# Merging small triangular inverses: one link of the dependent chain replaced, and banks of their own for two batches

## The chip, the cores and the metric

The kernel runs on one core of one Trainium2 chip. The metric is device time in microseconds (us) of that core. TensorE (PE) multiplies and writes PSUM, eight banks of 512 float32 columns on 128 partitions; ScalarE (ACT) and VectorE (DVE) read PSUM and copy to SBUF; GpSimd (POOL) works on SBUF alone; SyncE (SP) issues most DMAs.

## The reference, cut to what matters

Two layers on 512 tokens of width 1024: an RWKV-7 time mixer and a spatial gating unit, each followed by a SwiGLU FFN, with RMS norms around all. The change lies in the RWKV-7 mixer. Its recurrence, per head of width 64:

```
S_t = S_{t-1} diag(w_t) + (S_{t-1} a_t) b_t^T + v_t k_t^T ;   y_t = S_t r_t
```

The kernel computes it in chunks of 64 tokens. Within a chunk the tokens depend on each other through a strictly triangular 64x64 matrix L of a and b; the kernel needs (I - L)^-1 of every head and chunk, 16 heads x 8 chunks = 128 inverses. Everything is float32.

## The kernel before, in words

The 16 heads are taken in four batches b of four heads: two pairs q, and in a pair two heads hd, one on partitions 0 to 63, one on 64 to 127. With eight chunks that is 16 matrices u per hd and batch. A list `PLAN` (P0 E0 P1 ... F3 N0 B2 N1 B3 S2 N2 S3 N3) gives the order in which the program's steps are written: P projections, E the elementwise part, F `front` (products lm and bkt between the chunk's vectors, masked by GpSimd into LA, MV, BX), B `back` (the inverses, then products mp and gh that apply them), V values, S `scan` over the chunks (products us and Yp, small copies su), N group norm, bonus and gate. The order in which each engine really gets its instructions is decided by a planner that simulates the whole program while it is built, so steps of several batches interleave. It obeys data dependences, and dependences through buffers: `self.bank(tag, name)` hands out the PSUM banks of a tag in turn, and a new tile in a bank waits for the readers of the tile that had it before. In this phase tag pt is banks 3 and 4, pl is 1 and 2 (lm, bkt, mvt), mp is 5.

In `back`, LX and Dm give the inverses of the 16x16 diagonal blocks by a loop on VectorE (lines 1064 to 1070); Dn and Dt are two transposed forms of them (lines 1073, 1074). mvt are transposes of MV, copied to MVt (lines 1079 to 1084). Then the blocks are merged. With x = 0 or 1 for the upper or lower 32 rows of a matrix, `quarters` are the four (hd, x), each on 32 partitions of its own:

- Qp (line 1090), four quarters: off-diagonal part of L times Dn. Qs = Qp + I on VectorE (line 1093).
- Np (line 1099), x = 0 only, and Tp (line 1102), four quarters: Dt with Qs. Tp holds the 32x32 inverses, copied to the diagonal of bdT by VectorE and ScalarE (line 1107); Np is copied to Dn2 by ScalarE (line 1105).
- Q2p (line 1113): the 32x32 block of L below the diagonal times Dn2; copied to Q2 (lines 1116, 1117).
- T2p (line 1122): Q2 times the lower inverse in bdT, the off-diagonal 32x32 block; copied to bdT (line 1126). The last two copies are kept as `merged0`, `merged1`: loads for the out-projection are issued behind those of batch 3.

After that mp (line 1131) multiplies bdT with MVt, and gh (line 1138) with BX; VectorE adds gh into MV (lines 1140, 1141), which `scan` reads. One product of two 32x32 float32 tiles appears as two matmul instructions in the profile. In the profile's names Dn2 is Dn, Q2 is Q, Dn is hn, and id32 is id.

Of the kernel before, what the change touches and what calls it, by code (L numbers as in the profile page):

```python
# [13 lines left out]
P = 128  # L14
# [119 lines left out]
class Trunk:  # L134
# [553 lines left out]
    def rwkv(self, x0):  # L688
        nc, i, tc = self.nc, self.i, self.tc
        v, a, g = nc.vector, nc.scalar, nc.gpsimd  # L690
        mm = nc.tensor.matmul
        with ExitStack() as ctx:
# [352 lines left out]
            def back(b, o):  # L1045
# [40 lines left out]
                quarters = [(64 * hd + 32 * x, hd, x) for hd in q2 for x in q2]  # L1086
                Qp = self.bank("pt", "Qp")
# [6 lines left out]
                Np = self.bank("pt", "Np")  # L1094
                Tp = self.bank("pt", "Tp")
                for u in range(16):
                    for z, hd, x in quarters:
                        if x == 0:
                            mm(Np[z:z + 32, u * 32:(u + 1) * 32], Dt[z:z + 32, u, x, :], Qs[z:z + 32, u, :], start=True, stop=True)
                for u in range(16):  # L1100
                    for z, hd, x in quarters:
                        mm(Tp[z:z + 32, u * 32:(u + 1) * 32], Qs[z:z + 32, u, :], Dt[z:z + 32, u, x, :], start=True, stop=True)
                Dn2 = el("Dn2", (P, 16, 32))
                for z in (0, 64):
                    a.copy(Dn2[z:z + 32].rearrange("p u s -> p (u s)"), Np[z:z + 32, :])
                for z, hd, x in quarters:
                    (a.copy if x else v.tensor_copy)(bdT[z:z + 32, :, hd, 32 * x:32 * x + 32],
                                                     Tp[z:z + 32, :].rearrange("p (u t) -> p u t", t=32))

                Q2p = self.bank("pt", "Q2p")  # L1110
                for u in range(16):
                    for z in (0, 64):
                        mm(Q2p[z + 32:z + 64, u * 32:(u + 1) * 32], LAu[z:z + 32, u, 32:64], Dn2[z:z + 32, u, :],
                           start=True, stop=True)
                Q2 = el("Q2", (P, 16, 32))
                a.copy(Q2[32:64].rearrange("p u s -> p (u s)"), Q2p[32:64, :])
                v.tensor_copy(Q2[96:128].rearrange("p u s -> p (u s)"), Q2p[96:128, :])
                T2p = self.bank("pt", "T2p")
                for u in range(16):
                    for hd in q2:  # L1120
                        z = 64 * hd
# [348 lines left out]
```

## Time and profile before

| | |
|---|---|
| three runs, us | 1311.30, 1311.77, 1318.54 (median 1311.77) |
| profiled execution, its own time, us | 1310.66 |
| its span, us | 1309.0 |
| PE busy | 1255.0 us, 96%, 9692 matmuls |
| PE weight loads busy | 1090.5 us, 83% |
| DVE busy | 991.3 us, 76% |
| ACT busy | 739.0 us, 56% |
| POOL busy | 150.2 us, 11% |
| four merges in the span | from 221.0, 269.0, 313.6 and 359.4 us |

Busy PE is not PE at its peak, since the ends of pipelined matmuls are modelled. PEclk is the granted TensorE clock as a share of full speed. A bracket such as "[1.98 <-issue]" gives the idle time of the engine before an instruction and what ended it; "issue" is a wait for nothing that the profile shows. The releaser of a wait is inferred.

### The profile page before, as it was taken

The numbers are of one execution on the slowest core, as the hardware profiler recorded it, in microseconds if no ns is written. First come the engines' busy times: TensorE is split into PE (matmuls) and PEld (weight loads), VectorE is DVE, ScalarE is ACT, GpSimd is POOL, SyncE is SP. The second block draws the span as 40 slices with busy tenths as digits, with TensorE's granted clock in tenths as the row PEclk, the third lists the DMA queues.
The fourth block names the chain that finished last, engine by engine and source line by source line (L and its number), as shares of the span: only waits on it lengthen the run. The fifth ranks groups of instructions, "written<-read, shape, count | busy, mean of one in ns | idle before, by whom it ended". The sixth has DMA issues, their size and how long they took to land.

```text
span 1309.0 us, 24482 instructions
## 1 busy us (share of the span) xinstructions
PE 1255.0 (96%) x9692; PEld 1090.5 (83%) x9692; DVE 991.3 (76%) x1613; ACT 739.0 (56%) x1303; POOL 150.2 (11%) x300
## 2 busy tenths in 40 slices
PE   5999999989899999999999999999999999999997
PEld 3667799878777698999997878878898999998876
DVE  6976766467957779768779976575689777789985
ACT  7986785576454454445456556653464454455553
POOL 0000284566100012000000000020002000000000
PEclk9999999989989999999999999999999999999999
DMA  5137595322143225243344413242440433344322
GB/s 164 33 97 176 144 227 158 86 72 62 60 117 120 81 66 161 72 123 115 92 149 138 125 59 118 91 139 90 142 114 1 129 109 107 109 129 145 113 65 81
DMA packets 218819, 143.24 MB, mean 109 GB/s; under 512 B 67872, under 2 KB 193360, under 8 KB 218704
## 3 DMA queue, kind: packets, MB, share of 16 engines
q1 hardware_dynamic: 217408, 136.96, 36.6%
q0 software_dynamic: 1296, 4.72, 1.1%
q8 instruction: 76, 1.25, 0.4%
q14 instruction: 39, 0.32, 0.1%
HBM read 128.02 MB, written 13.63 MB: 108 GB/s over the span
## 4 chain that ended last, share of the span: by engine, by line
PE 67%; DVE 8%; issue 2%; ACT 1%; DMA 1%; SPq 0%; POOL 0%; DVEq 0%; ACTq 0%
PE acc L208 25%; PE Q L208 10%; PE Z L208 7%; PE gu L208 6%; PE R L208 6%; PE u L208 3%; PE gh L1138 1%; DVE wlo L184 1%; PE Yp L1180 1%; DVE wsum L413 1%; PE lm L1023 1%; PE mp L1131 1%; PE ptr L283 1%; DMA wq<-in_ffn_w_up_dram 1%; DVE x L339 1%
## 5 line engine op out<-in xcount | busy, mean ns | idle before, releaser
L208 PE MATMUL Q<-bc,whi 128*128 128x256 f32 x816 | 147.5, 281 | 2.9 <-ACT hn L457 2.9
L184 DVE TENSOR_TENSOR wlo<-wraw,whi 128x1024 fp32r<-128x1024 f32 x83 | 103.3, 1247 | 58.7 <-ACT whi L183 57.6
L208 PE MATMUL acc<-whi,ablk 128*128 128x512 f32 x448 | 141.5, 395 | 2.7 <-DVE acc L642 2.7
L183 ACT CAST whi<-wraw 128x1024 fp32r<-128x1024 f32 x83 | 86.9, 1049 | 92.7 <-PE acc L208 16.6
L208 PEld LDWEIGHTS Q<-bc,whi 128*128 128x128 f32 x816 | 125.6, 189 | 3.7 <-ACT hn L457 3.5
L183 ACT CAST whi<-wsum 128x1024 fp32r<-128x1024 f32 x68 | 71.0, 1051 | 86.3 <-PE Q L208 29.2
L208 PE MATMUL Q<-bc,wlo 128*128 128x256 f32 x408 | 114.5, 281 | 0.0
L208 PE MATMUL gu<-hT,whi 128*128 128x256 f32 (+1 forms) x480 | 109.1, 322 | 0.0
L208 PEld LDWEIGHTS acc<-whi,ablk 128*128 128x128 f32 x448 | 84.1, 188 | 23.3 <-ACT hn L640 1.8
L208 PE MATMUL Z<-bc,whi 128*128 128x256 f32 x544 | 99.9, 281 | 1.6 <-DVE bc L184 1.6
L208 PE MATMUL R<-bc,whi 128*128 128x256 f32 x544 | 99.0, 280 | 0.0
L184 DVE TENSOR_TENSOR wlo<-wsum,whi 128x1024 fp32r<-128x1024 f32 x68 | 82.1, 1220 | 18.9 <-ACT whi L183 17.7
L183 ACT CAST whi<-wq 128x1024 fp32r<-128x1024 f32 x51 | 53.5, 1049 | 70.2 <-PE R L208 22.9
L208 PE MATMUL acc<-wlo,ablk 128*128 128x512 f32 x224 | 88.7, 396 | 2.2 <-DVE wlo L184 2.2
L208 PEld LDWEIGHTS gu<-hT,whi 128*128 128x128 f32 x480 | 79.4, 188 | 8.1 <-issue 1.0
L208 PEld LDWEIGHTS Z<-bc,whi 128*128 128x128 f32 x544 | 84.1, 189 | 1.8 <-DVE bc L184 1.8
L184 DVE TENSOR_TENSOR wlo<-wq,whi 128x1024 fp32r<-128x1024 f32 x51 | 64.3, 1262 | 26.7 <-ACT whi L183 26.6
L208 PEld LDWEIGHTS R<-bc,whi 128*128 128x128 f32 x544 | 84.0, 188 | 0.4
L208 PE MATMUL proj<-xsp,whi 128*128 128x512 f32 x256 | 82.5, 401 | 1.3 <-ACT r L832 1.3
L208 PE MATMUL Z<-bc,wlo 128*128 128x256 f32 x272 | 76.6, 282 | 1.7 <-DVE wlo L184 1.7
L208 PEld LDWEIGHTS Q<-bc,wlo 128*128 128x128 f32 x408 | 77.2, 190 | 0.0
L208 PE MATMUL R<-bc,wlo 128*128 128x256 f32 x272 | 76.7, 282 | 0.0
(377 smaller groups left out, 3196.1 us busy)
## 6 DMA issues: line engine op xcount, KB each, us to landing
wc<-in_ffn_w_down_dram SPq DMA_DIRECT2D x38, 512.0 KB, 3.6
wq<-in_ffn_w_gate_dram SPq DMA_DIRECT2D x68, 256.0 KB, 4.1
wq<-in_ffn_w_up_dram SPq DMA_DIRECT2D x68, 256.0 KB
wraw<-in_rwkv_w_rkv_dram SPq DMA_DIRECT2D x24, 512.0 KB, 5.1
wraw<-in_sgu_w_in_dram SPq DMA_DIRECT2D x16, 512.0 KB, 4.2
wraw<-in_ffn_w_gate_dram SPq DMA_DIRECT2D x10, 512.0 KB, 4.5
wraw<-in_ffn_w_up_dram SPq DMA_DIRECT2D x10, 512.0 KB
x<-in_x_dram SPq DMA_DIRECT2D x8, 512.0 KB, 3.8
```

Source lines behind the costliest of these rows:

```text
L183: self.nc.scalar.copy(hi, src)
L184: self.nc.vector.tensor_tensor(lo, src, hi.bitcast(F32), op=ALU.subtract)
L208: self.nc.tensor.matmul(out, l, r, start=start, stop=stop, skip_group_check=resumed)
L283: self.nc.tensor.transpose(pt[:, j * P:(j + 1) * P], xt[:, kt * P:(kt + 1) * P], self.ident)
L339: v.scalar_tensor_tensor(xts[tt][:, c], f, y[:, 0:1], xts[tt][:, c], op0=ALU.mult, op1=ALU.add)
L413: v.tensor_tensor(s, x, y, op=ALU.add)
L1023: mm(lm[:, cc * P:(cc + 1) * P], st[:, cc].rearrange("p n t -> p (n t)"), mv[:, cc, :, hd, :], start=True, stop=True)
L1131: mm(mp[:, cc * P:(cc + 1) * P], bdT[:, q * NC + 4 * hh + cc].rearrange("p h t -> p (h t)"), mt[:, cc, :], start=True, stop=True)
L1138: mm(gh[:, cc * P:(cc + 1) * P], mt[rows, cc, :], bx[rows, 0:2, cc, :], start=True, stop=True)
L1180: mm(yp[yr, yc], MV[hh, q][:, cc, 1, hd, :], su[:, q, hd, :], start=True, stop=True)
```

## The change

The products are written in another order. A group Gp = Dn^T with the lower-left 32x32 block of L (x = 0 only) needs nothing of Qs and replaces Np; its copy is G, copied by ScalarE, or by both engines in batches 2 and 3. Q2p becomes G times Qs. Tp is cut into two calls of `turned(x)`, 32 products each: x = 1 ahead of Q2p, x = 0 after T2p; `placed(x, ...)` copies each to bdT, head 0 by ScalarE and head 1 by VectorE. So the dependent groups are Qp, Q2p, T2p where they were Qp, Np, Q2p, T2p. The number of products (224 a batch) and of PSUM reads (11 a batch) stays.

In batches 2 and 3 (`apart`) each group but Qp takes two banks, one for each head: Gp, Q2p and the x = 0 half of T from tag pl, the x = 1 half and T2p from tag pt. In batches 0 and 1 both heads share one bank of tag pt, as before.

```diff
+                tops = [(hd, 64 * hd) for hd in q2]
+                flat2 = lambda t: t.rearrange("p u s -> p (u s)")
+                apart = b >= 2
+
+                def pair(name, tag):
+                    if apart:
+                        return [self.bank(tag, name) for _ in tops]
+                    return [self.bank("pt", name)] * 2
+
+                def copies(dst, src):
+                    for hd, z in tops:
+                        last = (v.tensor_copy if hd else a.copy)(dst(hd, z), src(hd, z))
+                        o["merged" + str(hd)] = last
+
+                def turned(x):
+                    Tp = pair("Tp", "pt" if x else "pl")
+                    for u in range(16):
+                        for hd, z in tops:
+                            z += 32 * x
+                            mm(Tp[hd][z:z + 32, u * 32:(u + 1) * 32], Qs[z:z + 32, u, :], Dt[z:z + 32, u, x, :], start=True, stop=True)
+                    return Tp
+
+                def placed(x, Tp):
+                    at = slice(32 * x, 32 * x + 32)
+                    copies(lambda hd, z: bdT[z + 32 * x:z + 32 * x + 32, :, hd, at],
+                           lambda hd, z: Tp[hd][z + 32 * x:z + 32 * x + 32].rearrange("p (u t) -> p u t", t=32))
+
...
-                Np = self.bank("pt", "Np")
-                Tp = self.bank("pt", "Tp")
+                Gp = pair("Gp", "pl")
                 for u in range(16):
-                    for z, hd, x in quarters:
-                        if x == 0:
-                            mm(Np[z:z + 32, u * 32:(u + 1) * 32], Dt[z:z + 32, u, x, :], Qs[z:z + 32, u, :], start=True, stop=True)
+                    for hd, z in tops:
+                        mm(Gp[hd][z:z + 32, u * 32:(u + 1) * 32], Dn[z:z + 32, u, 0, :], LAu[z:z + 32, u, 32:64], start=True, stop=True)
+                G = el("G", (P, 16, 32))
+                for hd, z in tops:
+                    (v.tensor_copy if hd and apart else a.copy)(flat2(G[z:z + 32]), Gp[hd][z:z + 32, :])
+                T1 = turned(1)
+                Q2p = pair("Q2p", "pl")
                 for u in range(16):
-                    for z, hd, x in quarters:
-                        mm(Tp[z:z + 32, u * 32:(u + 1) * 32], Qs[z:z + 32, u, :], Dt[z:z + 32, u, x, :], start=True, stop=True)
-                Dn2 = el("Dn2", (P, 16, 32))
-                for z in (0, 64):
-                    a.copy(Dn2[z:z + 32].rearrange("p u s -> p (u s)"), Np[z:z + 32, :])
-                for z, hd, x in quarters:
-                    (a.copy if x else v.tensor_copy)(bdT[z:z + 32, :, hd, 32 * x:32 * x + 32],
-                                                     Tp[z:z + 32, :].rearrange("p (u t) -> p u t", t=32))
-                Q2p = self.bank("pt", "Q2p")
+                    for hd, z in tops:
+                        mm(Q2p[hd][z + 32:z + 64, u * 32:(u + 1) * 32], G[z:z + 32, u, :], Qs[z:z + 32, u, :], start=True, stop=True)
+                placed(1, T1)
+                Q2 = el("Q2", (P, 16, 32))
+                copies(lambda hd, z: flat2(Q2[z + 32:z + 64]), lambda hd, z: Q2p[hd][z + 32:z + 64, :])
+                T2p = pair("T2p", "pt")
                 for u in range(16):
-                    for z in (0, 64):
-                        mm(Q2p[z + 32:z + 64, u * 32:(u + 1) * 32], LAu[z:z + 32, u, 32:64], Dn2[z:z + 32, u, :],
+                    for hd, z in tops:
+                        mm(T2p[hd][z:z + 32, u * 32:(u + 1) * 32], Q2[z + 32:z + 64, u, :], bdT[z + 32:z + 64, u, hd, 32:64],
                            start=True, stop=True)
-                Q2 = el("Q2", (P, 16, 32))
-                a.copy(Q2[32:64].rearrange("p u s -> p (u s)"), Q2p[32:64, :])
-                v.tensor_copy(Q2[96:128].rearrange("p u s -> p (u s)"), Q2p[96:128, :])
-                T2p = self.bank("pt", "T2p")
...
+                placed(0, turned(0))
+                copies(lambda hd, z: bdT[z:z + 32, :, hd, 32:64], lambda hd, z: T2p[hd][z:z + 32].rearrange("p (u t) -> p u t", t=32))
```

More of the change, by code (lines that the diff above doesn't have):

```diff
@@ L1114, in back @@
                            start=True, stop=True)
-                Q2 = el("Q2", (P, 16, 32))
-                a.copy(Q2[32:64].rearrange("p u s -> p (u s)"), Q2p[32:64, :])
-                v.tensor_copy(Q2[96:128].rearrange("p u s -> p (u s)"), Q2p[96:128, :])
-                T2p = self.bank("pt", "T2p")
-                for u in range(16):
-                    for hd in q2:
-                        z = 64 * hd
-                        mm(T2p[z:z + 32, u * 32:(u + 1) * 32], Q2[z + 32:z + 64, u, :], bdT[z + 32:z + 64, u, hd, 32:64],
-                           start=True, stop=True)
@@ L1124, in back @@
-                for hd, cp in ((0, a.copy), (1, v.tensor_copy)):
-                    z = 64 * hd
-                    o["merged" + str(hd)] = cp(bdT[z:z + 32, :, hd, 32:64], T2p[z:z + 32, :].rearrange("p (u t) -> p u t", t=32))
+                placed(0, turned(0))
+                copies(lambda hd, z: bdT[z:z + 32, :, hd, 32:64], lambda hd, z: T2p[hd][z:z + 32].rearrange("p (u t) -> p u t", t=32))
                 for hh, q in units:
```

## The prediction

> **What bounds the kernel now.** I read the page first: its span, and the chain of work that ended last.
>
> ```profile
> span 1309.0 us, 24482 instructions
> ...
> PE 67%; DVE 8%; issue 2%; ACT 1%; DMA 1%; SPq 0%; POOL 0%; DVEq 0%; ACTq 0%
> ```
>
> The profiled execution took 1310.66 us by its own clock against this span of 1309.0, so 1.7 us lie around the span. The chain is two thirds TensorE (PE), so a microsecond on PE's path counts and one on another engine counts only where PE waits for it. Next, the busy time by stage: each row gives the stretch, its length, busy time with instruction count of PE, PE weight loads, VectorE (DVE), ScalarE (ACT) and GpSimd, then the granted PE clock, the DMA share and GB/s.
>
> ```profile
> 213.00:412.00 199.00, 185.38 (x3128) 162.12 (x3128) 132.02 (x294) 113.17 (x268) 70.37 (x169) 0.94 0.29 85
> 412.00:440.00 28.00, 24.66 (x150) 18.10 (x146) 20.51 (x40) 12.75 (x25) 0.00 (x0) 1.00 0.44 132
> 440.00:1309.00 869.00, 850.60 (x5365) 761.54 (x5364) 686.52 (x1041) 446.45 (x729) 34.81 (x31) 1.00 0.35 105
> ```
>
> The edited function runs in the first row's stretch. PE stands 199.00 - 185.38 = 13.6 us there, and the granted clock averages 0.94, worth another 0.06 x 199 = 11.9 us. The FFN and SGU stretch of 869 us contains none of the edited instructions, and its PE is 98% busy. So the change can matter by what it does to those two sums, and by work it adds to PE. The four merges, from the first product Qp to the first mp, and what follows the last:
>
> ```profile
> 220.90:237.90 17.00, 15.34 (x513) 14.64 (x512) 4.97 (x7) 5.57 (x13) 4.66 (x11) 0.90 0.11 35
> 269.00:287.80 18.80, 14.38 (x512) 13.14 (x512) 9.28 (x12) 13.14 (x33) 9.23 (x23) 0.91 0.23 57
> 313.60:340.50 26.90, 24.08 (x583) 20.29 (x581) 18.65 (x39) 21.03 (x54) 15.17 (x37) 0.94 0.24 73
> 359.40:375.50 16.10, 13.30 (x514) 12.27 (x513) 6.02 (x13) 8.32 (x19) 0.41 (x2) 0.74 0.19 55
> 375.50:412.00 36.50, 36.50 (x273) 29.31 (x273) 25.87 (x55) 16.11 (x34) 0.69 (x1) 0.97 0.49 145
> ```
>
> In the four, PE stands 1.66, 4.42, 2.82 and 2.80 us (length less the first busy column), 11.7 in all; the clock costs 0.10 x 17.0 + 0.09 x 18.8 + 0.06 x 26.9 + 0.26 x 16.1 = 9.2. The **ceiling of any gain** is therefore near 21 us, 1.6%. After the fourth merge PE is busy without a gap to 412 us, so what is won or lost before 375.5 passes straight on. The fourth merge, in order of time (start, length, engine, line, operation, count, and in brackets the idle time before it):
>
> ```profile
> 359.41 1.43 PE L1090 MATMUL Qp<-hn,LA 32*32 32x32 f32 x128
> ...
> 361.45 0.68 DVE L1093 TENSOR_TENSOR Qs<-Qp,id 128x512 f32<-128x512 f32 x1
> ...
> 362.19 1.16 PE L1099 MATMUL Np<-Qs,Dt 32*32 32x32 f32 x61 [0.51 <-DVE Qs L1093]
> ...
> 363.43 1.16 ACT L1105 COPY Dn<-Np 32x512 f32<-32x512 f32 x2 [0.57 <-PE Np L1099]
> ...
> 363.68 1.46 PE L1102 MATMUL Tp<-Dt,Qs 32*32 32x32 f32 x122 [0.23 <-issue]
> ...
> 365.19 0.68 DVE L1107 COPY bdT<-Tp 32x512 f32<-32x512 f32 x1 [2.87 <-PE Tp L1102]
> 365.90 0.58 ACT L1107 COPY bdT<-Tp 32x512 f32<-32x512 f32 x1 [1.31 <-DVE bdT L1107]
> 366.51 0.69 DVE L1107 COPY bdT<-Tp 32x512 f32<-32x512 f32 x1 [0.64 <-ACT bdT L1107]
> 367.23 1.80 PE L1113 MATMUL Q2p<-Dn,LA 32*32 32x32 f32 x59 [1.98 <-issue]
> ...
> 369.07 0.58 ACT L1116 COPY Q<-Q2p 32x512 f32<-32x512 f32 x1 [2.59 <-PE Q2p L1113]
> ...
> 370.02 0.70 DVE L1117 COPY Q<-Q2p 32x512 f32<-32x512 f32 x1
> ...
> 371.46 1.91 PE L1122 MATMUL T2p<-bdT,Q 32*32 32x32 f32 x62
> ...
> 373.41 0.57 ACT L1126 COPY bdT<-T2p 32x512 f32<-32x512 f32 x1 [0.96 <-PE T2p L1122]
> ...
> 374.02 0.69 DVE L1126 COPY bdT<-T2p 32x512 f32<-32x512 f32 x1 [2.16 <-ACT bdT L1126]
> ...
> 375.48 2.08 PE L1131 MATMUL mp<-MVt,bdT 128*128 128x128 f32 x8
> ```
>
> Two things are to be seen. The dependent groups are four: Qp, Np, Q2p, T2p, each followed by a copy out of PSUM. And the copies alternate: ACT's at 365.90 begins when DVE's ended, DVE's at 366.51 when ACT's did, DVE's at 374.02 when ACT's at 373.41 was through. The view of waits from 213 to 412 us has this as a rule, with PE's unexplained pauses beside it (engine, what waited for what, us in total, times, longest):
>
> ```profile
> DVE bdT L1126 <- ACT bdT L1126: 7.1, 2, 4.9
> ...
> PE Q2p L1113 <- issue: 3.7, 3, 2.0
> ...
> ACT bdT L1107 <- DVE bdT L1107: 3.8, 3, 1.9
> ...
> DVE bdT L1107 <- ACT bdT L1107: 2.0, 3, 0.7
> PE Tp L1102 <- issue: 1.8, 2, 1.6
> ```
>
> **The change, part by part.** *Work on PE.* Before and after a batch issues 7 x 32 products: Np's 32 go, Gp's 32 come, and Tp's 64 become two calls of 32. But a group's time hardly depends on its count: Qp, 128 instructions over four quarters, takes 1.43 us, Tp's 122 take 1.46, and Np, with half the count in two quarters, still 1.16. Splitting Tp therefore costs 2 x 1.16 - 1.46 = +0.86 a batch, 3.4 us in four if PE has no slack. If it falls into the pauses called "issue" (3.7 + 1.8 = 5.5 us, which sit inside Tp and Q2p, runs of hundreds of small products), it costs nothing. Ends: 0 and 3.4; I take 0 in the chains below, where the groups are already counted one by one, and 0 in batch 0, whose 1.66 us idle covers it.
>
> Those pauses I keep at their length, since the count of small products does not change. The Trainium skill, "Runtime: NRT & Kernel Launch", section "Instruction fetch mechanics", says that instructions come in blocks of 256 and that crossing a block is mostly hidden. That speaks against pauses that recur by count; by it the 1.98 us of the fourth merge need not come back and the time would be 2 us lower. The trace cannot say whether these pauses are fetches.
>
> *The chain, shared banks (batches 0 and 1).* Before, by the rows above: Qp 1.43, Qs 0.68, Np 1.16, Tp 1.46 (beside the two Dn2 copies, 1.16), Q2p at Np's 1.16, its copies 0.58 + 0.70, T2p 1.16, its copies 0.57 + 0.69: 9.6. After: Qp 1.43, Gp 1.16 (Qs runs under it), T1 1.16 (G's two ACT copies under it), Q2p 1.16, copies 1.28 in turn, T2p 1.16, then T0 1.16, which needs Q2p's bank and so cannot fill the copies' wait, and its copies 0.58 + 0.69: 9.8. (T1 and T0 are the two halves of Tp.) G's copies cost up to 1.16 a batch if something else keeps ScalarE from them under T1. The step saved behind Np comes back as T0 at the end: **0**. Bounds: -4.42 if all of batch 1's idle time goes, +1.7 if both batches pay the split.
>
> *The chain, own banks (batches 2 and 3).* Each head's copy has its engine and bank, so a pair takes 0.70 instead of about 1.27, and T0 has banks of its own and fills the wait for Q2. Qp 1.43, Gp 1.16, T1 1.16, Q2p 1.16, T0 1.16 (over Q2's 0.70), T2p 1.16, copies 0.69: 7.9, **-1.7** against 9.6. That presupposes that the alternation is due to the bank and not to the common destination (bdT, Q2). Two engines do write one tile at once:
>
> ```profile
> 308.56 0.76 ACT L1031 COPY BX<-lm 64x256 f32<-64x256 f32 x2 [1.47 <-DVE MV L1140]
> 308.59 0.83 POOL L1018 COPY BX<-ident 64x256 f32<-64x256 f32 x2 [3.52 <-DVE MV L1140]
> ```
>
> Both waited for the same release, the VectorE reader of BX, and ran side by side into that tile; what they don't share is a PSUM bank.
>
> In batch 3 nothing stands in the way, and I take the -1.7 whole. In batch 2 the new products' bank tag does. Gp, Q2p and T0 take tag pl, whose two banks also serve the next batch's lm and bkt and this batch's mvt, all asked for earlier in the program:
>
> ```profile
> 319.71 0.57 PE L1099 MATMUL Np<-Qs,Dt 32*32 32x32 f32 x24
> ...
> 336.12 0.57 ACT L1084 COPY MVt<-mvt 128x512 f32<-128x512 f32 x1
> 336.58 0.57 ACT L1126 COPY bdT<-T2p 32x512 f32<-32x512 f32 x1
> ...
> 339.75 0.69 DVE L1126 COPY bdT<-T2p 32x512 f32<-32x512 f32 x1
> ...
> 340.49 1.16 PE L1131 MATMUL mp<-MVt,bdT 128*128 128x128 f32 x8 [0.30 <-DVE bdT L1126]
> ```
>
> Today Np of batch 2 runs at 319.7 in tag pt, while the last mvt copy ends at 336.69. Gp can only follow that copy. From 336.69: 1.16 + 0.69 + 1.16 + 0.70 + 1.16 + 0.69 = 5.56, so 342.3 in place of 340.44: +1.8. Behind a waiting Gp on PE's queue stand whatever the planner put there, in batch 2 the scan's us and Yp and the transposes vt, and ScalarE and VectorE wait for those. If the order brings mvt forward by as much as its PE work allows, nothing is lost and 1.7 is won. VectorE also does six of the eleven copies in batches 2 and 3 instead of five, 0.69 each. I take **+0.7** for batch 2, that one copy, with ends -1.7 and +1.8 + 0.69 + 2.6; the last is a second wait like that of T2p's copy on DVE (ready at 337.15 when ACT's ended, begun at 339.75).
>
> The moved steps issue no DMA. SP's loads for the out-projection are ordered behind the last copy of batch 3's merge, as now, and move with its end.
>
> *The clock.* In the fourth merge:
>
> ```profile
> 363.70:367.10 3.40, 1.55 (x127) 1.45 (x128) 1.27 (x2) 1.46 (x3) 0.00 (x0) 1.00 0.14 34
> 367.10:370.50 3.40, 3.27 (x76) 3.08 (x76) 0.86 (x3) 1.38 (x4) 0.00 (x0) 0.53 0.02 5
> 370.50:373.90 3.40, 3.32 (x79) 3.00 (x79) 0.50 (x2) 1.66 (x6) 0.00 (x0) 0.50 0.24 70
> ```
>
> A stretch with PE busy for 1.55 of 3.40 us is followed by two at half clock although PE is busy 3.27 and 3.32 in them, mostly with small products. Fewer waits inside the merge should spare one such stretch in batch 3: half of 4.2, **-2.1**; ends 0 and -4.2. The same could happen in batch 1, and a new low stretch (0.5 x 3.4 = +1.7) could open anywhere since six groups of small products now follow one another; I take neither.
>
> The Trainium skill, "TensorE: Matmul & The Clock Gate", part 1, has the clock halve after an idle window of about 3.4 us and return after a busy one. The trace agrees on the halving and on the length; it disagrees on the return, for 3.27 and 3.32 busy of 3.40 did not bring it back. By the rule alone the whole 4.2 would go once the gaps close.
>
> Sum: 0 + 0 + 0.7 - 1.7 - 2.1 = -3.1, so 1307.6 against the execution's 1310.66. The median of the runs shown, 1311.77, lies 1.1 above that execution, which gives **1308.7** to be compared with it.
>
> **The rivals.** *G waits for the banks (slower).* In batch 2 the group that was to be free of the chain stands behind mvt's copies, and DVE, busy in 18.65 of 26.9 us, makes the second late copy: +1.8 + 0.69 + 2.6. With the split paid in all four batches, +3.4, and no clock gain, +8.5: 1320. It decides if batch 2's Gp starts after 336. For it: tags and order in the code, and DVE's late copy. Against it: mvt needs little and can be moved ahead.
>
> *The gaps close.* Batch 3 loses its idle time and its low clock, 2.8 + 4.2, batch 1 likewise, 4.42 + 1.7: -13.1, 1298.7. For it: the clock row of batch 3 (0.74) and the idle PE of batch 1. Against it: the pauses called "issue" remain, and the small products seemed not to raise the clock. It decides if both merges stay at 0.95 or above.
>
> *The change doesn't do what it says.* The copies alternate still, for the sake of the common destination: batch 3 gains nothing on its chain and keeps its clock, 1311.8. Against it stand the two BX rows.
>
> *The order is remade.* The instruction order of every engine comes from a planner that simulates the whole; another chain makes another order from the first merge to the out-projection, where loads of w_o and the scan compete. By the rows this can cost or win about what PE stands outside the merges from 213 to 440, 13.6 - 11.7 + 28.0 - 24.66 = 5.2, on top of the above; a tail beyond 1% on either side.
>
> **How the numbers follow.** Forecast 0.43; G waits 0.20; the gaps close 0.15; not as said 0.07; remade order 0.15. A change of this kernel's time within 1% (13.1 us) can't be told from none. Half of the gap-closing case and a quarter of the remade order lie below 1298.7: 0.11. Above 1324.9 lie a third of the remade order, 0.05, and a tenth of the bank wait, 0.02: 0.07. The rest, 0.82, is within. The range goes from the gap-closing case, 1298, to the bank wait, 1321; outside stay the remade order's tails and half of the gap-closing.
>
> **What would show it.** Right: Np gone and Gp under Qs; pairs of copies at the same time on ACT and DVE in batches 2 and 3 alone; mp of batch 3 about 14 us or less behind its Qp; PEclk of that merge above 0.85; PE pauses called "issue" of some 5 us again. Wrong: batch 2's Gp behind the mvt copies, T0 not filling Q2's wait, more stretches at 0.5, or differences that lie outside 213 to 440 us, which none of these steps explains.

## The result, and the profile after

The changed kernel takes 1328.61 us (1324.35 to 1329.88), the kernel before 1311.63 beside it: a ratio of 1.0122, 95% interval 1.0099 to 1.0145. It is **slower by 17 us**, outside the range and on the other side of the forecast.

The profiled execution took 1329.88 us against 1310.66 before, +19.2. First its stages, as before in the order length, PE, PE weight loads, VectorE, ScalarE, GpSimd, granted clock, DMA share, GB/s. The stretch now ends at the first gate/up product of the FFN (459.1 us before, 475.1 after), so that the same work lies inside.

```profile
213.00:459.10 246.10, 229.14 (x3360) 195.75 (x3360) 166.83 (x379) 135.67 (x325) 70.37 (x169) 0.95 0.30 86
```

That is the kernel before. The changed one, with its rest and its four merges:

```profile
span 1328.2 us, 24481 instructions
...
213.00:475.10 262.10, 243.08 (x3351) 209.32 (x3350) 168.34 (x379) 133.32 (x320) 67.25 (x166) 0.90 0.27 79
475.10:1328.00 852.90, 834.31 (x5275) 748.99 (x5273) 672.50 (x996) 436.87 (x697) 34.80 (x31) 0.99 0.36 107
219.80:237.00 17.20, 16.65 (x526) 15.79 (x526) 5.24 (x7) 7.12 (x17) 5.08 (x13) 1.00 0.12 34
265.90:288.90 23.00, 16.66 (x501) 15.10 (x500) 11.20 (x18) 14.33 (x34) 9.41 (x21) 0.74 0.20 53
321.60:352.40 30.80, 27.33 (x544) 24.42 (x545) 20.93 (x45) 16.53 (x41) 11.06 (x30) 0.77 0.17 49
373.60:390.50 16.90, 14.17 (x499) 13.31 (x497) 8.03 (x14) 8.21 (x18) 0.41 (x2) 0.66 0.26 76
```

The first merge, 17.2 us, is to be set against 19.3 and not against the 17.00 of the prediction's row: that row ends at 237.90, and the first mp of batch 0 runs at 240.33 (Qp at 220.99). The kernel before, up to there:

```profile
220.90:240.33 19.43, 17.77 (x534) 17.07 (x532) 4.97 (x7) 7.85 (x18) 5.76 (x14) 0.91 0.10 30
```

So the four merges together grew from 81.1 to 87.9 us. The rest of the 16.0 us lies between and behind them, most of it between batches 1 and 2, where 25.8 us with 224 PE instructions became 32.7 us with 264.

PE stands 262.1 - 243.1 = 19.0 us where it stood 17.0, and its count of instructions is the same. What grew is PE's busy time, by 13.9 us, at a clock of 0.90 in place of 0.95. So the time did not go into waits or work but into **half-rate clock**. In the trace the granted clock is either 1.0 or 0.5, and it changes only at the edges of a grid of 3.413 us. Cut at those edges, the second half of batch 2's merge reads:

```profile
331.40:334.81 3.41, 2.59 (x48) 2.04 (x42) 2.65 (x4) 3.07 (x9) 1.88 (x5) 1.00 0.58 172
334.81:338.23 3.42, 2.16 (x45) 1.68 (x44) 3.35 (x5) 2.57 (x4) 0.77 (x2) 0.99 0.04 11
338.23:341.64 3.41, 2.94 (x60) 2.81 (x54) 3.31 (x13) 0.68 (x2) 2.29 (x6) 0.50 0.41 122
341.64:345.06 3.42, 2.71 (x54) 2.58 (x53) 3.39 (x8) 0.58 (x1) 0.00 (x0) 0.50 0.11 37
345.06:348.47 3.41, 3.41 (x75) 3.41 (x73) 1.95 (x7) 0.57 (x1) 0.00 (x0) 0.50 0.00 0
348.47:351.88 3.41, 3.41 (x57) 3.35 (x55) 2.29 (x6) 0.61 (x2) 0.00 (x0) 0.50 0.02 5
351.88:355.30 3.42, 3.42 (x18) 3.42 (x17) 3.04 (x12) 1.24 (x2) 0.00 (x0) 0.51 0.00 0
355.30:358.71 3.41, 3.41 (x32) 3.07 (x30) 3.41 (x2) 0.90 (x2) 0.00 (x0) 1.00 0.00 0
```

One thin stretch (2.16 busy of 3.42) is followed by five at half rate, three of them with PE busy throughout. Each costs 1.71 us of PE's work. Up to the first gate/up product there were 7 such stretches before and there are 15 after; two more stand in the rest, where there were none (the last 5 us of both traces aside). Ten more stretches are 17.1 us, the 2.0 us of idle time make it 19.1 of the 19.2.

The parts of the change are all there. In batch 3 the copies run side by side, as forecast, but the merge is no shorter:

```profile
374.73 1.17 PE L1124 MATMUL Gp<-LA,hn 32*32 32x32 f32 x63
...
380.44 2.15 PE L1132 MATMUL Q2p<-Qs,G 32*32 32x32 f32 x64
382.68 0.58 ACT L1098 COPY Q<-Q2p 32x512 f32<-32x512 f32 x1 [1.23 <-PE Q2p L1132]
382.68 0.70 DVE L1098 COPY Q<-Q2p 32x512 f32<-32x512 f32 x1 [2.17 <-issue]
383.99 2.21 PE L1140 MATMUL T2p<-bdT,Q 32*32 32x32 f32 x61
...
386.15 1.74 PE L1106 MATMUL Tp<-Dt,Qs 32*32 32x32 f32 x58
...
389.84 0.57 ACT L1098 COPY bdT<-Tp 32x512 f32<-32x512 f32 x1
390.46 0.79 PE L1148 MATMUL mp<-MVt,bdT 128*128 128x128 f32 x2 [1.10 <-ACT bdT L1098]
```

A group of 32 products that takes 1.17 us at full rate takes 2.15 and 2.21 at half rate, and T0 (the last Tp) did not fill the wait for Q2: it runs after T2p, and its copy is the one that mp waits for. In batch 2 the rival of the bank wait came about, G behind the last mvt copies:

```profile
336.52 1.05 ACT L1084 COPY MVt<-mvt 128x512 f32<-128x512 f32 x2
337.14 2.76 PE L1124 MATMUL Gp<-LA,hn 32*32 32x32 f32 x64 [1.07 <-ACT MVt L1084]
...
340.37 3.43 PE L1132 MATMUL Q2p<-Qs,G 32*32 32x32 f32 x64 [0.47 <-ACT G L1127]
```

### The profile page after: what moved, and what is told of

Read it like the earlier page. It is cut to its first block, busy times and chain, and to the rows that moved or that the text cites. A ratio compares the mean times of both kernels' runs of the same rounds, so it can differ in the third digit from the quotient of the medians.

```text
span 1328.2 us, 24481 instructions
## 1 busy us (share of the span) xinstructions
PE 1272.1 (96%) x9692; PEld 1107.9 (83%) x9692; DVE 993.7 (75%) x1615; ACT 738.0 (56%) x1301; POOL 148.2 (11%) x300
## 4 chain that ended last, share of the span: by engine, by line
PE 79%; DVE 11%; DMA 3%; ACT 3%; issue 3%; SPq 1%; POOL 0%; DVEq 0%; ACTq 0%
PE acc L208 24%; PE Q L208 9%; PE proj L208 6%; PE gu L208 6%; PE Z L208 6%; PE R L208 6%; PE u L208 3%; PE v L208 3%; DVE wlo L184 2%; PE gh L1155 2%; PE lm L1023 2%; PE mp L1148 1%; PE lora L811 1%; DVE wsum L413 1%; PE Yp L1197 1%
## 5 line engine op out<-in xcount | busy, mean ns | idle before, releaser
L208 PE MATMUL Z<-bc,whi 128*128 128x256 f32 x544 | 102.6, 286 | 2.0 <-DVE bc L184 2.0
```

Of the source, the lines that this page charges most:

```text
L208: self.nc.tensor.matmul(out, l, r, start=start, stop=stop, skip_group_check=resumed)
```

## The experiments

All times are set against runs of the kernel before on the same chip. The accounts run from 213 us to the first gate/up product: half-rate stretches (1.71 us each) and PE's idle time. What remains, PE's work at full rate, is 210 to 220 us in all kernels without added products (before 217.2, after 217.5; low where PE idles inside a half-rate stretch). The time is the median of all executions, the account is that of the one profiled. Its own time lies within 1.7 us of the median but for three: 1329.3 us with the change in batch 0 alone, 1313.7 in batch 1 alone, and 1311.3 for the kernel before with its Q2 copies exchanged.

```
kernel                              us      ratio (95%)              stretches  idle
before                              1311.6  1                         7         17.0
after                               1328.6  1.0122 (1.0099-1.0145)   15         19.0
shared banks                        1318.1  1.0047 (1.0032-1.0063)   12         17.0
own banks, old order                1321.6  1.0076 (1.0049-1.0103)   14         18.9
own banks in batch 3 alone          1325.7  1.0096 (1.0076-1.0116)   15         19.1
mvt in another bank                 1334.0  1.0160 (1.0140-1.0179)   17         23.9
after + full-size products          1343.1  1.0224 (1.0201-1.0247)   16         16.8
before + full-size products         1330.4  1.0124 (1.0100-1.0149)    9         23.2
change in batch 0 alone             1324.7  1.0092 (1.0060-1.0124)   15         23.9
change in batch 1 alone             1317.9  1.0040 (1.0021-1.0058)    8         21.3
change in batch 2 alone             1329.5  1.0133 (1.0096-1.0170)   15         18.1
change in batch 3 alone             1320.5  1.0067 (1.0036-1.0097)   14         21.3
before, Q2 copies exchanged         1314.9  1.0023 (1.0005-1.0040)    8         17.2
before, T2 copies exchanged         1327.8  1.0121 (1.0106-1.0136)   17         23.4
before, T copies exchanged          1325.0  1.0095 (1.0079-1.0112)   15         21.0
after, all pairs exchanged          1338.4  1.0201 (1.0185-1.0216)   20         23.1
after, Q2 copies exchanged          1332.7  1.0156 (1.0127-1.0185)   16         24.0
after, batch 2 in mp and pf         1327.4  1.0101 (1.0063-1.0139)   16         19.7
the same, Q2 copies exchanged       1330.1  1.0138 (1.0114-1.0162)   15         23.0
```

### What halves the clock

A kernel of products alone, in which `small` issues 32x32 products and `full` 128x128 ones:

```python
A = bank("A", "p"); full(A, 4); small(A, 384, two); close(A, "A")
warm()
B = bank("B", "p"); full(B, 4); small(B, 192, four); close(B, "B")
warm()
Cc = bank("C", "p"); full(Cc, 4); small(Cc, 256, two, every=8); close(Cc, "C")
```

> Leaves out the whole computation: only phases of products, between runs of 64 full-size 128x128 products. A: 768 small 32x32 products over two quarters; B: 768 over four quarters; C: 512 small with a full-size one after every 16; D, E, F: a pause of some 5 us (a chain of VectorE copies), then 768 small, or 512 small with a full-size one after every 16, or 64 full-size products; G: ten groups of 32 small products, each behind the copies of the one before; H: the same with four full-size products in each wait. Theory 1: A and B fall to a granted clock of about 0.5 after one stretch of 3.4 us though PE has no gap, D stays at 0.5 to its end, C stays at 1.0, E and F come back to 1.0 within about 4 us, G lies near 0.5, H near 1.0. If only idle time lowers the clock: A and B stay at 1.0 and D comes back after about 4 us, like F; G falls and H does not.

PE's order came out so that full-size products stand in the intended pauses and in the waits of G, which makes those phases mixed ones too. Phase A begins at 28.3 us; its full-size products are back from 71.4 us on. The stretches of the grid around both, then the waits of PE:

```profile
25.48:28.90 3.42, 3.42 (x61) 3.30 (x61) 0.00 (x0) 0.00 (x0) 0.00 (x0) 1.00 0.00 0
28.90:32.31 3.41, 2.40 (x151) 2.29 (x145) 0.00 (x0) 0.00 (x0) 0.00 (x0) 1.00 0.02 5
32.31:35.73 3.42, 3.36 (x130) 3.23 (x124) 0.00 (x0) 0.00 (x0) 0.00 (x0) 0.50 0.02 5
35.73:39.14 3.41, 3.41 (x134) 3.41 (x132) 0.00 (x0) 0.00 (x0) 0.00 (x0) 0.50 0.02 5
...
69.85:73.27 3.42, 3.42 (x68) 3.35 (x65) 0.00 (x0) 0.58 (x1) 0.00 (x0) 0.50 0.02 5
73.27:76.68 3.41, 3.41 (x18) 3.41 (x18) 0.00 (x0) 0.00 (x0) 0.00 (x0) 0.50 0.00 0
76.68:80.09 3.41, 3.41 (x32) 3.41 (x32) 0.00 (x0) 0.00 (x0) 0.00 (x0) 1.00 0.00 0
```

```profile
PE B L42 <- issue: 20.5, 11, 2.2
...
PE D L42 <- issue: 3.1, 4, 1.2
PE A L42 <- issue: 1.4, 2, 1.0
```

In A the clock halves behind a stretch of small products with PE busy for 2.40 of 3.41 us, and small products alone do not bring it back: A stays at half rate from 32.31 to 76.68 us, 13 stretches, though 35.73:39.14 is busy from end to end. One stretch full of full-size products at half rate (73.27:76.68) brings it back. C and E, with 16 small products to one full-size one, and G and H, stay at 1.0 throughout. So theory 1 holds for A to D and H; E and F never left full rate, and the low clock expected of G did not come, because G had full-size products between its groups.

How much is needed can be counted. In each stretch of this run and of five others (before, after, and the next three) I counted PE's records by shape and fitted one weight to each shape. A stretch is followed by full rate if its weights sum to 1, with 0.078 for a 128x128 record, 0.051 for a 64-row one, 0.0286 for a 128x64 one, and 0.0052, **a fifteenth**, for a 32x32 one (its share of the array is a sixteenth). That is 12.8 full-size records; a stretch at full rate holds 27 at 0.125 us each (phase W: 192 in 24.0 us), at half rate 13.6. So by this fit about half of what the array can do at full rate must be used. At half rate only a stretch nearly full of full-size products reaches that, and a mixed one doesn't: one thin stretch therefore costs several. On the fourteen later runs, which had no part in the fit, the weights, with those of the wider products, sort over 99% of some 5300 stretches rightly and foretell nearly all of the some 220 that ran at half rate; to call every stretch fast would be right in 96%. It is a rule fitted to these runs, no more.

Phase B shows what the pauses called "issue" are:

```profile
94.86 1.93 PE L42 MATMUL B<-x,ident 32*32 32x32 f32 x128 [2.18 <-issue]
98.86 1.93 PE L42 MATMUL B<-x,ident 32*32 32x32 f32 x128 [2.08 <-issue]
102.59 1.93 PE L42 MATMUL B<-x,ident 32*32 32x32 f32 x128 [1.80 <-issue]
...
q8 instruction: 11, 0.18, 1.5%
```

The first three rows are the timeline, the last the DMA queues from 85 to 131 us. Each run is of 128 records, which with their weight loads are 256 instructions; it is used up in 1.93 us, and the next comes 3.7 to 4.0 us after the last. In the same time the instruction queue moved 11 packets, 0.18 MB, 16 KB each. A block of 256 instructions thus takes 3.7 to 4.0 us to arrive when the one before is spent faster. A merge has 224 products of 4 instructions, 3.5 blocks: an estimate of 13 to 14 us at least. No merge of batch 3 in any run took less than 15.5 us. The Trainium skill, "Runtime: NRT & Kernel Launch", "Instruction fetch mechanics", has the crossing mostly hidden; for small products the trace disagrees, by 1.8 to 2.2 us a block.

Full-size products against the low clock, in the changed kernel inside each group, two of them, and in the kernel before ahead of Q2p and T2p, four each, in batches 1 to 3:

```diff
+                def warm(u, ps):
+                    if u % 8 == 0:
+                        mm(ps[0][:, u * 32:u * 32 + P], self.ident, self.ones, start=True, stop=True)
...
+                fill(4, Qs)
                 Q2p = self.bank("pt", "Q2p")
...
+                fill(4, Qs)
                 T2p = self.bank("pt", "T2p")
```

> The changed kernel with two full-size 128x128 products added to each group of small ones (48 more in all, written to the group's own bank and overwritten at once). They add up to 48 x 0.29 = 14 us of PE work. Theory 1 (small products alone do not bring the clock back): the low-clock loss falls from 25.8 us to below 14 us, and the time stays about where it was or falls, 1315 to 1330 us, although the work grew. If the loss has another cause, such as the pauses ahead of the groups: the loss stays at 22 us or more and the time rises to 1335-1345 us.

> The kernel before, with four full-size 128x128 products ahead of Q2p and four ahead of T2p in batches 1 to 3 (24 more, 24 x 0.275 = 6.6 us of PE work, into the bank of tag mp, read by nobody), where PE waits. Theory (a stretch of 3.413 us whose products fill less than about half of the array's time halves the clock of the next; a small product counts about a fifteenth of a full-size one): the low-clock loss up to the first gate/up product falls from 11.9 us to 6 or less, and the time is 1305 to 1312 us although PE has 6.6 us more to do. If full-size products in the waits do not hold the clock: loss 11 us or more and 1313 to 1319 us.

Neither paid. The merge of batch 3 of the first, then that of batch 1 of the second:

```profile
378.90:400.20 21.30, 18.21 (x513) 15.38 (x513) 11.45 (x18) 10.30 (x20) 0.41 (x2) 0.92 0.36 109
```

```profile
270.20:289.30 19.10, 14.26 (x521) 12.75 (x521) 9.60 (x13) 12.11 (x30) 9.01 (x20) 1.00 0.21 56
```

Where they stand the clock is higher: batch 3 of the changed kernel goes from 0.66 to 0.92, though its merge grows from 16.9 to 21.3 us, and batch 1 of the kernel before from 0.91 to 1.00, which that merge also reached without them (below). But the whole has 16 stretches (27.3 us) and 9 (15.4 us), not fewer: in the first, batches 1 and 2 still fell and, being mixed, could not come back at half rate, and in both the order of everything else moved. By its numbers the first run met its second expectation. The second run's clock loss, 15.4 us, is that of its second expectation, but its time of 1330 us meets neither, with 6 us of its idle time new.

### Order or banks

```diff
-                apart = b >= 2
+                apart = False
```

> The changed kernel's order of products (G first, T0 last) with one shared bank per group in all four batches, tag pt, as before the change. Theory 1 (the clock: runs of small products that follow one another keep the clock at half rate, and the new order makes such runs): still slow, 1324 to 1332 us, and the sum of (1 - clock) x length from 213 us to the first gate/up product of the FFN stays near the changed kernel's 25.8 us (before: 12.0). Theory 2 (the bank wait: Gp in tag pl stands behind the mvt copies in batch 2): Gp of batch 2 no longer waits for an mvt copy, the merge of batch 2 falls from 30.9 us to 27 or less, and the time to 1316-1324 us. Theory 3 (the planner remade the whole order): no number, a time anywhere from 1305 to 1335 us with the landmarks of batches 0 to 2 moved by microseconds either way.

The kernel before with a bank per head in batches 2 and 3. This run also gives copies to other engines there: each copy of head 0 goes to ScalarE, each of head 1 to VectorE.

```diff
-                Np = self.bank("pt", "Np")
-                Tp = self.bank("pt", "Tp")
+                Np = pair("Np", "pl")
+                Tp = pair("Tp", "pt")
```

> The kernel before with its own order (Np, Tp, Q2p, T2p) but a bank per head in batches 2 and 3 (Np and Q2p in tag pl, Tp and T2p in tag pt; head 0 copied by ScalarE, head 1 by VectorE). Theory 1 (the new order makes the low clock): 1306 to 1313 us, low-clock loss about the 12 us of before, and the copies of batch 3 side by side, worth up to -1.7 us. Theory 2 (bank wait in batch 2): Np of batch 2 stands behind the last mvt copy and the time is 1315 to 1325 us although the order is the old one. Theory 3: anywhere from 1305 to 1330 us, with landmarks moved in batches 0 and 1 too, whose code is the same as before.

Two runs of the changed kernel: own banks in batch 3 alone, and mvt of batch 2 moved:

```diff
+                apart = b == 3
...
+                        pt = self.bank("mp" if b == 2 else "pl", "mvt")
```

> The changed kernel with banks of their own in batch 3 alone; batch 2 shares one bank per group as batches 0 and 1 do. If the wait of batch 2's G product for the mvt copies' banks makes the second half of the loss: batch 2's merge comes back from 30.8 us to about the 23.5 us of the run with shared banks and loses no clock, and the time is 1314 to 1320 us. If own banks cost as such, by taking tag pl from the next work, batch 3 has none behind it, so the same. If batch 2's loss came from the order of products: 1325 us or more.

> The changed kernel with the mvt transposes of batch 2 written to the bank of tag mp in place of tag pl; own banks in batches 2 and 3 stay. If the wait for mvt's banks is the cause: Gp of batch 2 runs right behind Qp, as it does in batch 3, the merge takes 24 us or less, and the time is 1314 to 1321 us. If taking both banks of tag pl holds up the next batch's lm and bkt, so that other work moves: batch 3's Qp stays at 370 us or later and the time is 1323 us or more.

The merges of batches 1 and 2 with shared banks, then that of batch 2 in the old order with own banks:

```profile
268.10:290.20 22.10, 18.77 (x502) 17.05 (x501) 11.28 (x18) 14.05 (x34) 9.10 (x21) 0.61 0.21 60
322.20:345.70 23.50, 19.94 (x552) 16.77 (x552) 16.18 (x32) 17.87 (x43) 10.90 (x29) 1.00 0.23 64
```

```profile
312.20:344.90 32.70, 29.24 (x585) 25.78 (x585) 23.87 (x54) 20.98 (x52) 15.21 (x37) 0.80 0.20 60
```

Theory 2 holds: 23.5 us at full clock without own banks (the same with own banks in batch 3 alone), 30.8 to 32.7 with them in either order, and both times, 1318 and 1322 us, lie within its expectation. But each alone is slower than before, and the run with own banks in batch 3 alone, whose batch 2 is as short, takes 1325.7 and not the 1314 to 1320 expected of it: what it won there it lost behind the last merge, 92.0 us from there to the first gate/up product where before took 83.6. With mvt away G still waited 1.0 us, now for a copy of bkt, which holds the same banks for the next batch. Its merge of 27.4 us and its Qp of batch 3 at 369.3 meet neither expectation, its time that of the second; that run says nothing on banks as such.

### The change in one batch at a time

```diff
+                if b == 3:
                     Qp = self.bank("pt", "Qp")
                     ...
+                else:
+                    (the merge of before)
```

and likewise for 0, 1 and 2. Up to the changed merge the program's order is that of before.

> The new order of products in batch 0 alone, where full-size products of v stand between the groups; batches 1 to 3 as before the change. If the new order is harmful only where no full-size work stands between its groups: batch 0's merge takes 17.2 to 19.3 us and the time is 1308 to 1313 us. If the new order costs wherever it is (one more product group at the end of the chain): 1314 us or more.

> The new order of products (shared banks, as in the change) in batch 1 alone. Up to 269 us the order is that of before. If the new order itself lowers the clock where little full-size work stands between its groups: batch 1's merge takes 21.5 to 23.5 us in place of 18.8, with a low-clock loss of 5 to 9 us in place of 1.7. If only the planner's later order costs: 18 to 20 us for this merge, and any loss lies behind it. Whole time 1311 to 1328 us either way.

> The new order and the own banks in batch 2 alone. If the wait for the mvt copies is the change's own: Gp of batch 2 starts behind the last mvt copy and the merge takes 30 to 33 us in place of 26.9, with a low-clock loss of 5 us or more. If it came from the history of the changed batches 0 and 1: 24 to 27.5 us. Whole time 1312 to 1328 us either way.

> The new order and the own banks in batch 3 alone, where the prediction took -1.7 us for the chain and -2.1 for the clock. By the prediction: the merge takes 14.4 us or less in place of 16.1, and the time is 1308 us. If the merge is bound by the arrival of its 896 instructions in blocks of 256, some 3.7 us each (3.5 x 3.7 = 13 us, whatever the chain): 15.5 to 17 us for the merge, low-clock loss 5 to 6 us, and 1311 to 1316 us, if the order behind it stays.

The merge of batch 0, of batch 1, of batch 2 with what follows it up to the next Qp, and of batch 3 with what follows it, each from its own run:

```profile
220.30:237.80 17.50, 16.59 (x525) 15.74 (x525) 5.56 (x7) 7.08 (x17) 5.03 (x12) 1.00 0.11 34
```

```profile
268.20:286.30 18.10, 14.81 (x512) 13.80 (x513) 9.52 (x13) 12.63 (x32) 9.22 (x22) 0.91 0.23 61
```

```profile
314.40:343.60 29.20, 26.40 (x573) 23.01 (x572) 20.48 (x42) 20.32 (x51) 15.25 (x37) 0.88 0.22 67
343.60:374.50 30.90, 28.87 (x161) 24.60 (x161) 16.61 (x39) 6.10 (x12) 0.00 (x0) 0.67 0.03 11
```

```profile
359.50:375.00 15.50, 13.31 (x481) 12.44 (x480) 7.66 (x13) 7.84 (x15) 0.00 (x0) 0.62 0.18 53
375.00:470.00 95.00, 85.75 (x536) 68.29 (x537) 59.44 (x141) 38.66 (x94) 1.10 (x3) 0.90 0.34 101
404.20:411.00 6.80, 2.90 (x27) 2.13 (x26) 4.02 (x12) 2.78 (x6) 0.00 (x0) 0.75 0.81 252
431.50:438.30 6.80, 3.85 (x13) 2.51 (x14) 5.27 (x13) 1.82 (x3) 0.00 (x0) 0.75 0.52 154
```

The changed merges alone take 17.5 us for 19.3 in batch 0, 18.1 for 18.8 in batch 1, 15.5 for 16.1 in batch 3, and 29.3 for 26.9 in batch 2, with Gp again behind mvt copies: together -0.7 us. How much of that is the change? In the runs with batch 2 alone and with batch 3 alone, batch 1's merge is still that of before, with the same order of instructions on PE, ScalarE and VectorE:

```profile
271.69:288.56 16.87, 12.98 (x513) 11.71 (x513) 9.60 (x13) 13.15 (x33) 9.85 (x23) 1.00 0.25 67
268.77:288.12 19.35, 16.99 (x513) 15.90 (x513) 9.58 (x13) 13.10 (x33) 9.01 (x22) 0.74 0.20 56
```

The same work took 16.9 and 19.4 us, 18.8 in the kernel before, with the clock at 1.00, 0.74 and 0.91. So in a single profile a merge's time is uncertain by more than a microsecond, and the gains in batches 1 and 3 are not shown. That in batch 0 is: 17.1 to 19.3 us in nine profiles with the new order there, 19.2 to 20.8 in nine with the old, all without products added to that merge. Nor does the 0.91 of batch 1 alone clear the new order of the low clock. In all eight profiles in which batches 0 and 1 both have it, batch 1's merge takes 21.7 to 23.1 us at 0.61 to 0.78; what makes the difference to batch 1 alone is not shown.

**Each of the four kernels is slower, by 6 to 17 us, and most of the loss lies behind the changed merge.** In batch 0 the merge came as its first expectation says and the time as its second; batch 1 came as its second says; in batches 2 and 3 the time is above all that was expected. Behind batch 2's merge the products up to the next Qp keep PE busy for 28.9 us at a clock of 0.67, where the kernel before took 17.9 at 1.00 for nearly the same number. In the run with batch 3 alone the merge hands over at 375.0, half a microsecond earlier than before, and the rest takes 95.0 us in place of 83.6. In it are two pairs of stretches in which PE has little to do (2.90 and 3.85 busy of 6.80), and the second of each pair and the stretch behind it ran at half rate: around 405 the transposes of the last batch wait for VectorE, around 432 the last gate products do. In the kernel before products of the out-projection stood beside both. Here they run before the first wait (to 402) and after it (from 414.2), and at the second they in turn wait for their weights (436.4). That the full-size products which can stand in a wait are a fixed stock, so that what fills one wait is missing in another, would fit this; no run tried it. In batch 3 the merge took 15.5 us and not the 14.4 of the prediction. Length and clock loss (5.9 us) are what the expectation by the arrival of instructions gave, but its floor is 13 us, and PE stood only 2.2 us: that the arrival sets the length is not shown.

### Exchanges that change no work

Two engines trade copies; products, banks and the number of copies stay.

```diff
-                a.copy(Q2[32:64].rearrange("p u s -> p (u s)"), Q2p[32:64, :])
-                v.tensor_copy(Q2[96:128].rearrange("p u s -> p (u s)"), Q2p[96:128, :])
+                v.tensor_copy(Q2[32:64].rearrange("p u s -> p (u s)"), Q2p[32:64, :])
+                a.copy(Q2[96:128].rearrange("p u s -> p (u s)"), Q2p[96:128, :])
...
-                for hd, cp in ((0, a.copy), (1, v.tensor_copy)):
+                for hd, cp in ((0, v.tensor_copy), (1, a.copy)):
...
-                    (a.copy if x else v.tensor_copy)(bdT
+                    (v.tensor_copy if x else a.copy)(bdT
```

> The kernel before, with its two Q2 copies exchanged between the engines (head 0 by VectorE, head 1 by ScalarE) in all four batches; the same products, banks and number of copies. If the change is slower because the planner lays out everything from the first merge on anew, and the order before was a good one out of many: this lands off 1312 us like the other variants, 1317 to 1330 us, with the low-clock loss and idle time up to the first gate/up product above 35 us (before 28.9). If the loss is a matter of the merge's own products and banks: 1309 to 1315 us.

> The kernel before, with its two last copies of a merge (T2p to bdT) exchanged between the engines: head 0 by VectorE, head 1 by ScalarE. Same two expectations: 1317 to 1330 us and low-clock loss plus idle time above 35 us if it is the planner's whole order, 1309 to 1315 us if it is the merge's own products and banks.

> The kernel before, with its four Tp copies exchanged between the engines: those of x = 0 by ScalarE, those of x = 1 by VectorE. Same two expectations: 1317 to 1330 us if it is the planner's whole order, 1309 to 1315 us if it is the merge's own products and banks.

And in the changed kernel, in all pairs of `copies`, then in Q2's alone:

```diff
-                        last = (v.tensor_copy if hd else a.copy)(dst(hd, z), src(hd, z))
+                        last = (a.copy if hd else v.tensor_copy)(dst(hd, z), src(hd, z))
```

> The changed kernel, with the copies of T1, Q2, T0 and T2 exchanged between the engines (head 0 by VectorE, head 1 by ScalarE); G's copies as they are. If the planner's order decides: anywhere from 1312 to 1335 us, as likely under 1322 us as over it. If the change's own products and banks cost 17 us: 1325 to 1333 us, with batch 2's G product behind the mvt copies again and that merge 30 us long.

> The changed kernel with its two Q2 copies exchanged between the engines in all batches; same products, banks and number of copies. If the 17 us are the change's own: 1325 to 1332 us. If they are one draw of the planner's order: anywhere from 1312 to 1340 us, off 1328.6 by 5 us or more.

The kernel before loses 3, 16 and 13 us to an exchange of equal work; the first lies within its second expectation, the two others within their first, nearly as slow as the change itself. The changed one loses 10 and 4 more, the one above both expectations, the other less than 1 us outside both. With the T2 copies exchanged the four merges take 81.9 us, 81.1 before; the loss lies behind the last of them, 95.3 us for 83.7:

```profile
379.95:475.20 95.25, 87.46 (x488) 68.31 (x487) 60.71 (x139) 39.45 (x90) 0.69 (x1) 0.88 0.33 104
```

**So an exchange of equal work, through the order that the planner then makes, can cost this kernel 16 us, about as much as the change.** That the 17 us of the change are of this kind, beyond the part of batch 2, is inferred from it and not shown. The kernel before has the fewest stretches and the shortest time of all 19 versions that do the whole work.

### Banks that nobody holds

```diff
-                        return [self.bank(tag, name) for _ in tops]
+                        return [self.bank(x, name) for x in (("mp", "pf") if tag == "pl" and b == 2 else (tag, tag))]
```

> The changed kernel, with G, Q2p and T0 of batch 2 in the banks of tags mp and pf, one per head, in place of the two of tag pl; batch 3 keeps pl. If batch 2 loses its time because its G product waits for the banks of pl (held by mvt in the changed kernel, by the next batch's bkt where mvt was moved away): G no longer waits for a copy of MVt or BX, the merge of batch 2 takes 27 us or less, Qp of batch 3 starts at 360 to 367 us, and the whole takes 1312 to 1327 us. If own banks cost as such: Qp of batch 3 at 369 us or later and 1328 us or more.

> As the run before, with the two Q2 copies exchanged between the engines, a second draw of the planner's order for equal work. Same expectations: Qp of batch 3 at 360 to 367 us and 1312 to 1327 us if it is the banks of pl, 369 us or later and 1328 us or more if own banks cost as such.

Batch 2's merge and what follows the last merge, in the first of the two:

```profile
322.20:343.70 21.50, 21.48 (x544) 18.70 (x545) 13.65 (x22) 15.89 (x40) 11.89 (x30) 0.96 0.25 70
380.50:475.10 94.60, 87.20 (x520) 68.33 (x521) 59.29 (x140) 37.89 (x91) 0.69 (x1) 0.88 0.32 101
```

The merge is the shortest batch 2 of all, 21.5 us with PE at work throughout, and Qp of batch 3 starts at 364.5 and 363.3 us (373.6 in the changed kernel): the wait for the banks of tag pl is shown as the cause of that part. (It isn't the only way to a long batch 2: the merge of before took 25.5 to 30.0 us there in other runs without added products.) The whole is no faster, 1327 and 1330 us: 94.6 us behind the last merge in place of 83.6. The expectation for the whole failed with the one for the merge fulfilled.

What stays open: the eight versions with own banks in batch 2 take 1321.6 to 1338.4 us, mean 1330.3, the nine without (and without added products) 1311.6 to 1327.8, mean 1320.7. The groups overlap, but their means lie 10 us apart, and these last two runs show that this is not the wait for pl alone. No version beat the kernel before.

## Why the prediction was wrong

*Work on PE: right.* Splitting Tp cost nothing that the account shows (217.2 and 217.5 us of work at full rate).

*The chain in shared banks: right alone, not together.* Taken 0, with bounds of -4.42 and +1.7. Alone, batch 0 gained 1.8 and batch 1 0.7, the latter within the scatter. In the changed kernel batch 0 took -2.1 and batch 1 +4.2, 23.0 us for 18.8, and the clock fell from 0.91 to 0.74 there. The row of 17.00 us for batch 0 stopped 2.4 us short of mp; the idle time of 1.66 is the same for the full 19.43, so the sums do not suffer.

*The chain in own banks, batch 3: the copies right, the sum not.* The copies ran side by side, so the change does what it says. Of the -1.7, alone at most -0.6 came, within the scatter; in the changed kernel it was +0.8. T0 did not fill the wait for Q2, and the time per group was not 1.16 us: at half rate a group takes 2.2. The chain of 9.6 us was also only part of a merge of 16.1; what stood beside it, the low clock and the pauses, decided. The pauses called "issue" were rightly kept: 4.7 us again (us 2.1, Gp 2.0, Tp 0.6); phase B ties pauses of this kind to the arrival of instructions.

*Batch 2: the forecast put the bank wait at nothing, its rival had it.* Taken +0.7, one copy, with an end at +5.1; alone it is +2.4, in the changed kernel 30.8 for 26.9, +4.0. The rival of the bank wait named the sign, and its condition was fulfilled: Gp at 337.14 where it decides from 336 on. Its 8.5 us, 3.4 of them for the split that cost nothing, were half of the loss.

*The clock: the step that failed.* The forecast took one low stretch less in batch 3, -2.1 with ends 0 and -4.2, and no new one anywhere. In batch 3 the loss grew, from 4.2 to 0.34 x 16.9 = 5.7, and in the whole there are ten stretches more: +17.1 us. The prediction had the rows that told against it: two stretches busy for 3.27 and 3.32 us stayed at half rate. From these it should have concluded that small products do not bring the clock back, and so that fewer waits inside a merge need not help there. It also named the new low stretches, at 1.7 us each, and left them out. The Trainium skill, "TensorE: Matmul & The Clock Gate", part 1, gave the length of the stretch; that a busy stretch brings the clock back holds in these traces only if full-size products fill it.

*The remade order: the rival that fits best, priced too low.* It was given 0.15 and 5.2 us, PE's idle time outside the merges. Exchanges of equal work show up to 16. That it makes up what the bank wait leaves of the 17 us stays inferred. The price left out that a wait laid bare also costs the clock behind it, 1.7 us and often a multiple.

Of the signs of being wrong that were named in advance, three came true: Gp behind the mvt copies, T0 not filling the wait for Q2, and more stretches at 0.5. The fourth did in part, with two of the ten stretches behind 475 us.

## What to carry to other kernels

Count the half-rate stretches before anything else: when PE's busy time grows with an unchanged count of instructions, look at the clock, not at the chain. Small products in a wait do not keep the clock up, and a shorter chain in one place may only move a bare wait to another. Where an order is planned as a whole, time a few versions that exchange equal work first: a change whose effect is inside their scatter (here 16 us, 1.2%) can't be judged by its one time.

## What was not expected of the hardware

The clock changes at the edges of a fixed grid of 3.413 us, and the place of the program on it differs from run to run. One order of instructions gives times 9 us apart (1311.3 to 1320.0 us in ten runs with the Q2 copies exchanged, 1309.5 to 1318.6 for the kernel before beside it), and up to 15 us (1317.6 to 1332.9 in six runs with the change in batch 0 alone). With shared banks PE's order up to batch 2 is that of the changed kernel, and still batch 1's merge ran at 0.61 there and at 0.74 here; in the order of before it ran at 0.74, 0.91 and 1.00. That the place of the grid makes the difference was not tried by itself. By the fit a 32x32 product counts a fifteenth of a full-size one for the clock. In phase B a block of 256 instructions took 3.7 to 4.0 us to arrive, twice the 1.93 us in which PE spent it.
